# Stores of decay matrices, feed-forward blocks and scaled rows: issued by the engine that makes the data instead of SyncE

## The chip, the cores and the metric

The kernel runs on one core of one Trainium2 chip. TensorE (PE) multiplies matrices; VectorE (DVE), ScalarE (ACT) and GpSimd (POOL) work element by element; SyncE (SP) issues transfers (DMAs) between the device's memory (DRAM) and the on-chip buffer. Any of SP, ACT and POOL can issue a DMA, and each engine executes its own instructions strictly in order: an instruction that waits for a semaphore holds up everything behind it on that engine. The metric is the time of one execution in device microseconds (us), as the median of several runs.

## What is computed

The program is a two-layer network on a sequence of 1024 rows of width 1024, in float32. Each layer is a mixer (a gated delta rule, "GDN", in layer 0; retention in layer 1), a layer norm, a convolutional feed-forward network of hidden width 2816, and another layer norm. Cut to what the change touches:

```python
def conv_ffn(h, w_up, conv_w, conv_b, w_down):
    gate, up = jnp.split(h @ w_up, 2, axis=-1)
    gate = causal_dwconv(gate, conv_w) + conv_b
    return (jax.nn.silu(gate) * up) @ w_down

for i in range(DEPTH):
    sh1, sc1, g1, sh2, sc2, g2 = jnp.split(mod, 6, axis=-1)
    y = mixers[i % N_MIXERS](x * (1.0 + sc1) + sh1)
    x = layer_norm(DN_ALPHA * x + (1.0 + g1) * y, ln_g[i, 0], ln_b[i, 0])
    y = conv_ffn(x * (1.0 + sc2) + sh2, ffn_up[i], ...)
    x = layer_norm(DN_ALPHA * x + (1.0 + g2) * y, ln_g[i, 1], ln_b[i, 1])
# in the gated delta rule:
    decay = jnp.where(causal, jnp.exp(jnp.where(causal, diff, 0.0)), 0.0)
```

## The kernel before

**Stages**, by the profiled execution's time: the GDN mixer (0 to about 580 us), its output projection (to 770), feed-forward up of layer 0 (770 to 1170), feed-forward down (to 1440), retention's input projections (to 1715), retention's core (to 2040), its output projection (to 2230), a transition in which the inputs of the next product are built (to 2290), feed-forward up of layer 1 (2290 to 2690), feed-forward down (to 2840), and the last layer norm (to 2894).

**Feed-forward up** (`layer_tail`, `strassen`, `wino`). The hidden width is taken in 11 pairs `fp` of 256 columns. Each pair has a gate item and an up item, and each item is one 2x2 block product in the Strassen-Winograd form: seven products of blocks instead of eight. An item loads two weight tiles `wr` of 128x1024 (L1357 for a11 and a12, L1358 for a21 and a22); the pool holds two such tiles, so each load waits until the last reader of the same buffer is done. DVE makes sums of weight blocks (L1346, `mm<-wr`), and every weight block, raw or summed, is split into a high and a low part by ScalarE (L89) and DVE (L90) before PE multiplies with it (L110 to L112). Raw blocks appear as `wb<-wr`, summed ones as `wb<-mm`; the last read of a `wr` buffer is such a DVE split or an L1346. ScalarE also copies products (L1362, `pc`).

A gate item's results are added up into `g` (L1723), and `conv_q` makes four quarter blocks `o` from them: ScalarE scales (L1732), DVE adds two shifted rows (L1737, twice), ScalarE applies SiLU (L1738). The up item multiplies each `o` by its result (L1760). Then four more blocks S1 to S4 are made in place in the same four `o` buffers, by GpSimd (L1768) except in the first pair. The feed-forward down product will read seven blocks per pair: 11, 12, 22 and S1 to S4. Each is written to DRAM by `store` (L1749): 7 x 11 x 2 layers = 154 stores of 256 KB. The `o` buffers come from the pool `qkv` of 20 buffers, 16 of which hold the right-hand blocks during this stage, so the next pair's L1732 can only begin when a store of the present pair has landed.

**Background.** While PE multiplies, a queue of background steps loads columns of the modulation weights (`mvw`, L227) and scales the residual rows `xg` (two GpSimd instructions L411 and L412, then a store by GpSimd itself, L413).

**GDN.** `t_decay` makes one decay matrix `U` per head: ScalarE applies exp (L841), and a 512 KB store puts it into DRAM (`Ld`, L842), from which 16 reads (L1038) take it later. There are eight heads.

**Retention.** `gain_step` (16 times with a store) scales residual rows on GpSimd (L2050, L2051) and stores them (L2052). It runs between the steps of the core; there GpSimd also makes the power function of each chunk's variance (L1976), for which DVE waits.

**What sets the order.** The program is written in a planned order, but the order on each engine is set when it is built, by a list scheduler that plays the program through with its own costs for every instruction. So a changed cost on one engine can move instructions on all of them. Loads wait in SP's queue in program order.

Of the kernel before, what the change touches and what calls it, by code (L numbers as in the profile page):

```python
# [26 lines left out]
ABLK = ("11", "12", "22", "S1", "S2", "S3", "S4")  # L27
# [6 lines left out]
def trunk_kernel(ctx: ExitStack, tc, A):  # L34
    nc = tc.nc
    pe, act, dve, pool, sp = nc.tensor, nc.scalar, nc.vector, nc.gpsimd, nc.sync
# [9 lines left out]
    def tl(tag, shape, dt=F32, name=None):  # L46
        return sb.tile(shape, dt, tag=tag, name=name or tag, bufs=BUFS[tag])
# [31 lines left out]
    def flat(ap):  # L79
        return ap.rearrange("p a b -> p (a b)")  # L80

    def hs(half):
        return slice(half * HALF, (half + 1) * HALF)
# [10 lines left out]
    def after(key):  # L94
        return tc.issue_after(anchor[key].ins) if key in anchor else nullcontext()
# [295 lines left out]
    xg = [dr.tile([S, D], F32, tag=f"xg{i}", name=f"xg{i}") for i in range(3)]  # L391
# [306 lines left out]
    U, DT, R, St = {}, {}, {}, {}  # L698
# [22 lines left out]
    def after_ev(*names):  # L721
        return ("ev", names)

    def emit(name, lat=0.0):
        events[name] = clk[0] + lat
# [45 lines left out]
    def take(tag, n):  # L771
        while free[tag] < n:
            yield lambda: free[tag] >= n
        free[tag] -= n
# [40 lines left out]
    Ld = dr.tile([GH, P, S], F32, tag="Ld", name="Ld")  # L815
# [3 lines left out]
    def decay(h):  # L819
        home = "auh" if h > 3 else "t2"  # L820
        for q4 in range(2):
            yield from take(home, 2)
            gm = [tl(home, [P, 4, P], F32R, name="gm") for _ in range(2)]
            for t, g in zip(gm, (gh64, gl64)):
                pool.tensor_tensor(t, bm(m_incl, 4), bc(g[:, q4s(q4), h], P), ALU.mult)
            yield LAT["gm"]
            pt = acc_tile() if h > 3 else sc_tile()
            pm(pt, m_lowr, gm[1], start=True, stop=False)
            pm(pt, m_lowr, gm[0], start=False, stop=True)
            dve.tensor_tensor(U[h][:, q4s(q4)], v4(pt), bm(mneg, 4), ALU.add)  # L830
            give(home, 2)

    def t_decay(p):
        yield after_ev(("g",), ("DD", p - 1), ("T", p // 2 - 1))
        for h in pairs[p]:
            yield from take("aux", 1)
            U[h] = tl("aux", [P, NCH, P], name="U")
            yield from decay(h)
        yield LAT["mm"]
        for h in pairs[p]:  # L840
            act.activation(flat(U[h]), flat(U[h]), AF.Exp)  # L841
            sp.dma_start(Ld[h], flat(U[h]))  # L842
        emit(("DD", p), LAT["exp"])

    def t_path(g):
# [383 lines left out]
    c, z = "c", "z"  # L1229
# [5 lines left out]
    for p in range(4):  # L1235
        q = p & 2
        todo += [(q + 0.28, t_decay(p)), (q + 0.2, t_chain(p)), (q + 0.25, prep(p)), (q + 0.22, dt_half(p, 0)), (q + 0.24, dt_half(p, 1)),
                 (q + 0.0 + p % 2 * 0.1, scan(p, pairs[p][0])), (q + 0.05 + p % 2 * 0.1, scan(p, pairs[p][1]))]
# [442 lines left out]
    def layer_tail(i, mix, wout, xsrc, x_mid, x_out, ln_next, final):  # L1681
# [25 lines left out]
        ad = dr.tile([NF // 2, 7, P, HALF], F32, tag=f"ad{i}", name=f"ad{i}")  # L1707
# [4 lines left out]
        def pair_items(fp):  # L1712
            g, o = [], {}

            def gate_start():
                g.extend(tl("lane", [P, D], name="g") for _ in range(2))

                def gate(q, a, b):
                    dst = g[q // 2][:, hs(q % 2)]
                    if b is None:  # L1720
                        act.activation(dst, a, AF.Copy)
                    else:
                        dve.tensor_tensor(dst, a, b, ALU.add)  # L1723
                return gate

            def conv_q(q):
                f, hf = 2 * fp + q // 2, q % 2
                gv = g[q // 2]
                w = cw[:, 3 * f:3 * f + 3]
                t = tl("qkv", [P, HALF], name="o")  # L1730
                with after("sp") if fp == 0 else nullcontext():
                    act.activation(t, gv[:, hs(hf)], AF.Copy, scale=w[:, 2:3])  # L1732
                for j in (1, 2):
                    c0 = HALF if hf else j
                    c1 = HALF * (hf + 1)
                    tv = t[:, c0 - HALF * hf:]
                    dve.scalar_tensor_tensor(tv, gv[:, c0 - j:c1 - j], w[:, 2 - j:3 - j], tv, ALU.mult, ALU.add)  # L1737
                act.activation(t, t, AF.Silu, bias=cb[:, f:f + 1])  # L1738
                o[q] = t

            def conv():
                for q in (1, 3, 0, 2) if fp == 0 else range(4):
                    if fp < 2:
                        late.append(lambda q=q: conv_q(q))
                    else:
                        conv_q(q)

            def store(nm, q):
                sp.dma_start(ad[fp, ABLK.index(nm)], o[q])  # L1749

            def up_start():
                seen = []

                def gated(q, a, b):
                    while q not in o:
                        late.pop(0)()
                    c = a
                    if b is not None:
                        dve.tensor_tensor(c, a, b, ALU.add)
                    dve.tensor_tensor(o[q], o[q], c, ALU.mult)  # L1760
                    if q != 1:
                        store({0: "11", 2: "12", 3: "22"}[q], q)
                    seen.append(q)
                    if len(seen) == 4:
                        for d, x, y, op, nm in ((1, 1, 3, ALU.add, "S1"), (0, 1, 0, ALU.subtract, "S2"),
                                                (2, 2, 0, ALU.subtract, "S4"), (3, 3, 0, ALU.subtract, "S3")):
                            def one(d=d, x=x, y=y, op=op, nm=nm):
                                (dve if fp == 0 else pool).tensor_tensor(o[d], o[x], o[y], op)  # L1768
                                store(nm, d)
                            if fp == 0:  # L1770
                                late.append(one)
                            else:
                                one()
                return gated

            return [(up[4 * fp], up[4 * fp + 2], gate_start, conv), (up[4 * fp + 1], up[4 * fp + 3], up_start, None)]
# [93 lines left out]
    for t in range(4):  # L1870
        x = tl("cv", [P, 516], name="xlo")[:, 0:HALF]
# [175 lines left out]
    def gain_step(m):  # L2047
        if gx:
            x, c, rs, gb = gx.pop()
            pool.tensor_tensor(x, x, gb[0], ALU.mult)  # L2050
            pool.tensor_tensor(x, x, gb[1], ALU.add)  # L2051
            sp.dma_start(xg[0][rs, hs(c)], x)  # L2052
        if m < 2 * NCH:
            c, r = divmod(m, NCH)
            if r == 0:
                gbs.append([tl("auh", [P, HALF], name="gb") for _ in range(2)])
                for t, nm in zip(gbs[-1], ("ln_g", "ln_b")):
                    sp.dma_start(t, A[nm][1:2, hs(c)].to_broadcast([P, HALF]))
            rs = slice(r * P, r * P + P)
            x = tl("lane", [P, HALF], name="xg")  # L2060
            sp.dma_start(x, xs[1][rs, hs(c)])
            gx.append((x, c, rs, gbs[-1]))

    gbs = []
    gains += [lambda m=m: gain_step(m) for m in range(2 * NCH + 1)]
    events["core", -1] = clk[0]
    free["qkv"] = 20
# [106 lines left out]
```

## Time and profile before

| | |
|---|---|
| median of 3 runs | 2893.8 us (2892.51 to 2897.38) |
| the profiled execution | 2895.86 us, of which its span is 2894.1 us |
| PE clock | 0.989 of full speed, mean over the span |
| PE busy | 2796.1 us (97%) |
| DVE busy | 2180.7 us (75%) |
| ACT busy | 1295.6 us (45%) |
| POOL busy | 487.1 us (17%) |
| DMA | 465.30 MB, mean 161 GB/s; 42.8% of the 16 DMA engines' time in the queues that SP and ACT feed, 0.8% in the one that POOL feeds |

An engine's busy time is the time in which at least one of its recorded instructions ran, without the instructions that issue DMAs on SP and ACT, the waits and the branches. A row of a timeline is: start in us, duration in us, engine, line, operation, the tiles written and read, their shapes, and in square brackets the idle time just before the instruction and what ended it. A row of the list of waits is: the waiting engine and line, what it waited for, then the total in us, the number of waits and the longest. "SPq" is SyncE's queue of DMA issues.

### The profile page before, as it was taken

How to read it: one execution, taken by the hardware profiler on the slowest of the kernel's cores; microseconds unless marked ns; L12 is line 12 of the kernel's file. 1: busy time of each engine (PE TensorE's matmuls, PEld its weight loads, DVE VectorE, ACT ScalarE, POOL GpSimd, SP SyncE). 2: the span in 40 equal slices, each digit the busy share in tenths (PEclk: the TensorE clock that was granted, in tenths of full speed). 3: DMA queues.
4: the chain of work that ended last, by engine and by line, in shares of the span. 5: the costliest groups of instructions: out<-in, count | busy, mean ns of one | idle time of the engine just before them, and what ended most of it. 6: DMA issues, size and time to landing. Idle time of an engine off the chain costs nothing.

```text
span 2894.1 us, 38921 instructions
## 1 busy us (share of the span) xinstructions
PE 2796.1 (97%) x13594; PEld 2287.9 (79%) x13594; DVE 2180.7 (75%) x3874; ACT 1295.6 (45%) x2387; POOL 487.1 (17%) x509
## 2 busy tenths in 40 slices
PE   8999999999999999999999999999999999999997
PEld 6787888877788778887888887777777788888886
DVE  5787688676788888868687656666688887777779
ACT  4663465344654444545333342222244644444543
POOL 0311221000023233000000002333201023332001
PEclk9999999999999999999999999999999999999999
DMA  7223243164254555855343364665754154434853
GB/s 277 88 95 121 91 137 99 52 240 153 95 189 164 193 182 171 295 154 189 126 148 120 120 200 151 198 207 172 245 195 146 62 197 138 142 129 164 289 182 117
DMA packets 252884, 465.30 MB, mean 161 GB/s; under 512 B 24144, under 2 KB 77776, under 8 KB 252688
## 3 DMA queue, kind: packets, MB, share of 16 engines
q1 hardware_dynamic: 218560, 408.02, 42.8%
q10 hardware_dynamic: 31488, 46.15, 4.3%
q0 software_dynamic: 2640, 8.65, 0.8%
q8 instruction: 107, 1.75, 0.3%
q14 instruction: 89, 0.73, 0.1%
HBM read 346.86 MB, written 115.87 MB: 160 GB/s over the span
## 4 chain that ended last, share of the span: by engine, by line
PE 54%; DVE 23%; DMA 12%; ACT 5%; issue 5%; POOL 1%; SPq 0%; ACTq 0%; DVEq 0%; POOLq 0%
PE acc L716 8%; PE acc L1292 5%; PE acc L1592 4%; PE acc L110 4%; PE acc L111 4%; PE acc L112 4%; PE sc L716 4%; DMA mvw<-in_ada_w 3%; PE sc L1292 3%; PE mm L716 2%; DVE o L1737 2%; DVE wb L90 2%; DMA wr<-in_ffn_up 2%; DVE qkv L490 2%; DVE mm L1346 2%
## 5 line engine op out<-in xcount | busy, mean ns | idle before, releaser
L716 PE MATMUL acc<-hT,wh 128*128 128x512 f32 x960 | 301.3, 396 | 0.0
L1592 PE MATMUL acc<-bb,ab 128*128 128x512 f32 x984 | 232.5, 396 | 7.1 <-DVE ab L90 3.7
L89 ACT ACTIVATE ab<-ar 128x512 fp32r<-128x512 f32 x210 | 131.1, 630 | 222.8 <-PE mm L303 49.8
L1592 PEld LDWEIGHTS acc<-bb,ab 128*128 128x128 f32 x984 | 185.6, 190 | 49.0 <-DVE bb L90 4.1
L716 PEld LDWEIGHTS acc<-hT,wh 128*128 128x128 f32 x960 | 183.7, 191 | 36.1
L90 DVE TENSOR_TENSOR ab<-ar,ab 128x512 fp32r<-128x512 f32 x210 | 147.8, 710 | 83.0 <-ACT ab L89 83.0
L1292 PE MATMUL acc<-T,wb 128*128 128x512 f32 x840 | 202.0, 390 | 0.4 <-DVE wb L90 0.4
L716 PE MATMUL acc<-hT,wl 128*128 128x512 f32 x480 | 197.9, 412 | 3.5 <-ACT sq L509 2.4
L89 ACT ACTIVATE wb<-mm 128x512 fp32r<-128x512 f32 x216 | 124.3, 597 | 169.5 <-DVE mm L1346 155.2
L1292 PEld LDWEIGHTS acc<-T,wb 128*128 128x128 f32 x840 | 157.6, 188 | 33.7 <-ACT o L1738 1.2
L90 DVE TENSOR_TENSOR wl<-wr,wh 128x1024 fp32r<-128x1024 f32 x98 | 124.6, 1272 | 76.5 <-ACT wh L89 72.8
L89 ACT ACTIVATE wh<-wr 128x1024 fp32r<-128x1024 f32 x98 | 103.6, 1060 | 138.3 <-PE acc L716 53.5
L90 DVE TENSOR_TENSOR wb<-wr,wb 128x512 fp32r<-128x512 f32 x162 | 115.8, 716 | 62.9 <-ACT wb L89 62.9
L1768 POOL TENSOR_TENSOR o<-o 128x512 f32<-128x512 f32 x80 | 113.4, 1426 | 267.4 <-ACT pc L1362 176.3
L1737 DVE SCALAR_TENSOR_TENSOR o<-g,vc,o 128x512 f32<-128x512 f32 (+2 forms) x176 | 149.6, 860 | 8.6 <-ACT o L1732 7.4
L90 DVE TENSOR_TENSOR wb<-mm,wb 128x512 fp32r<-128x512 f32 x216 | 145.2, 685 | 7.6 <-ACT wb L89 7.6
L89 ACT ACTIVATE wb<-wr 128x512 fp32r<-128x512 f32 x162 | 101.1, 626 | 92.7 <-PE acc L1292 27.9
L1346 DVE TENSOR_TENSOR mm<-wr 128x512 f32<-128x512 f32 x108 | 85.8, 794 | 74.5 <-DMA wr<-in_ffn_up 60.9
L716 PE MATMUL acc<-wh,hT 128*128 128x512 f32 x384 | 134.4, 412 | 1.8 <-DVE vv L90 1.8
L1362 ACT ACTIVATE pc<-acc 128x512 f32<-128x512 f32 x143 | 84.3, 590 | 108.7 <-PE acc L1292 63.0
L239 DVE SCALAR_TENSOR_TENSOR ada<-mvw,e,ada 128x512 f32<-128x512 f32 x140 | 106.0, 757 | 26.0 <-DMA mvw<-in_ada_w 25.7
L110 PE MATMUL acc<-T,wb 128*128 128x512 f32 x292 | 114.5, 392 | 5.2 <-DVE wb L90 5.1
(674 smaller groups left out, 7369.9 us busy)
## 6 DMA issues: line engine op xcount, KB each, us to landing
wr<-in_ffn_up SPq DMA_DIRECT2D x92, 512.0 KB, 3.9
mvw<-in_ada_w SPq DMA_DIRECT2D x80, 512.0 KB, 4.3
ad<-o SPq DMA_DIRECT2D x154, 256.0 KB, 2.3
ar<-ad SPq DMA_DIRECT2D x154, 256.0 KB, 3.8
Br<-in_ffn_down SPq DMA_DIRECT2D x88, 256.0 KB, 3.4
wr<-in_ret_wv SPq DMA_DIRECT2D x32, 512.0 KB, 3.6
ar<-od SPq DMA_DIRECT2D x56, 256.0 KB, 4.8
wr<-in_gdn_wqkv SPq DMA_DIRECT2D x24, 512.0 KB, 3.6
```

The costliest lines, as they stand in the source:

```text
L89: anchor["sp"] = act.activation(dst_h, src, AF.Copy)
L90: eng.tensor_tensor(dst_l, src, dst_h, ALU.subtract)
L110: mm(acc, wl[:, k], hl[0], start=first, stop=False)
L111: mm(acc, wh[:, k], hl[1], start=False, stop=False)
L112: mm(acc, wh[:, k], hl[0], start=False, stop=last)
L239: dve.scalar_tensor_tensor(a, wr[:, kk], e[:, k:k + 1], a, ALU.mult, ALU.add)
L716: pq(pe.matmul(out, lhsT, rhs, start=start, stop=stop), cost or COST[out.shape[-1]])
L1292: return pe.matmul(*a, skip_group_check=True, **kw)
L1346: dve.tensor_tensor(t, x, y, op)
L1592: return pe.matmul(*args, skip_group_check=True, **kw)
L1737: dve.scalar_tensor_tensor(tv, gv[:, c0 - j:c1 - j], w[:, 2 - j:3 - j], tv, ALU.mult, ALU.add)
L1768: (dve if fp == 0 else pool).tensor_tensor(o[d], o[x], o[y], op)
```

## The change

Three lines name another engine as the issuer of a store. No arithmetic, no buffer and no transfer is added or taken away.

```diff
@@ t_decay
         for h in pairs[p]:
             act.activation(flat(U[h]), flat(U[h]), AF.Exp)
-            sp.dma_start(Ld[h], flat(U[h]))
+            act.dma_start(Ld[h], flat(U[h]))
         emit(("DD", p), LAT["exp"])
@@ pair_items
             def store(nm, q):
-                sp.dma_start(ad[fp, ABLK.index(nm)], o[q])
+                pool.dma_start(ad[fp, ABLK.index(nm)], o[q])
@@ gain_step
             pool.tensor_tensor(x, x, gb[0], ALU.mult)
             pool.tensor_tensor(x, x, gb[1], ALU.add)
-            sp.dma_start(xg[0][rs, hs(c)], x)
+            pool.dma_start(xg[0][rs, hs(c)], x)
```

The list scheduler moves other instructions too. GpSimd's queue over one pair of feed-forward up in layer 0 (L411 to L413 are two background gains, L1768 the blocks S1 to S4) was:

```order
L411 TENSOR_TENSOR xg<-xg,gb 128x512
L412 TENSOR_TENSOR xg<-xg,gb 128x512
L413 DMA xg_161<-xg 128x512
L411 TENSOR_TENSOR xg<-xg,gb 128x512
L412 TENSOR_TENSOR xg<-xg,gb 128x512
L413 DMA xg_161<-xg 128x512
L1768 TENSOR_TENSOR o<-o 128x512 x4
```

and is now, over the part of a pair from the first gain's store on:

```order
L413 DMA xg_161<-xg 128x512
L1749 DMA ad_6811<-o 128x512
L411 TENSOR_TENSOR xg<-xg,gb 128x512
L412 TENSOR_TENSOR xg<-xg,gb 128x512
L413 DMA xg_161<-xg 128x512
L1749 DMA ad_6811<-o 128x512
L1768 TENSOR_TENSOR o<-o 128x512
L1749 DMA ad_6811<-o 128x512 x2
L1768 TENSOR_TENSOR o<-o 128x512
L1749 DMA ad_6811<-o 128x512
L1768 TENSOR_TENSOR o<-o 128x512 x2
L1749 DMA ad_6811<-o 128x512 x2
```

The seven stores of a pair now stand in GpSimd's queue, five of them between and behind its four L1768.

On DVE, at the end of an up item in the same stage (`wb<-wr` in L90 is the split of a raw weight block, whose end lets the next item's load L1358 begin; the two L1737 are the next pair's convolution), the difference is:

```order
 L1723 TENSOR_TENSOR g<-sc,pc 128x512
 L90 TENSOR_TENSOR wb<-mm,wb 128x512
-L1737 SCALAR_TENSOR_TENSOR o<-g,vc,o 128x511
-L1737 SCALAR_TENSOR_TENSOR o<-g,vc,o 128x510
-L90 TENSOR_TENSOR wb<-wr,wb 128x512 x2
+L90 TENSOR_TENSOR wb<-wr,wb 128x512
+L1737 SCALAR_TENSOR_TENSOR o<-g,vc,o 128x511
+L1737 SCALAR_TENSOR_TENSOR o<-g,vc,o 128x510
+L90 TENSOR_TENSOR wb<-wr,wb 128x512
 L1346 TENSOR_TENSOR mm<-wr 128x512
```

The first of the two splits has moved ahead of the two L1737. The same is found in most pairs of both layers.

On ScalarE, at the same place (`mm` and `wr` as on DVE; L1732 and L1738 are the convolution's first and last step), the difference is:

```order
 L89 ACTIVATE wb<-mm 128x512 x2
-L1732 ACTIVATE o<-g,vc 128x512
-L1362 ACTIVATE pc<-acc 128x512
-L89 ACTIVATE wb<-wr 128x512
-L1738 ACTIVATE o<-o,vc 128x512
+L1362 ACTIVATE pc<-acc 128x512
+L89 ACTIVATE wb<-wr 128x512
+L1732 ACTIVATE o<-g,vc 128x512
 L1362 ACTIVATE pc<-sc 128x512
 L89 ACTIVATE wb<-wr 128x512
 L251 ACTIVATE ada,cs<-mm 128x128 x4
+L1738 ACTIVATE o<-o,vc 128x512
```

L1732, which needs an `o` buffer that a store has left, has moved behind the copy L1362 and the split L89, and L1738 behind the next pair of these.

## The prediction

> **What bounds the kernel now.** I began with the page's totals, then took the chain that ended last, then the stages in which the moved stores lie.
>
> ```profile
> span 2894.1 us, 38921 instructions
> PE 2796.1 (97%) x13594; PEld 2287.9 (79%) x13594; DVE 2180.7 (75%) x3874; ACT 1295.6 (45%) x2387; POOL 487.1 (17%) x509
> PE 54%; DVE 23%; DMA 12%; ACT 5%; issue 5%; POOL 1%; SPq 0%; ACTq 0%; DVEq 0%; POOLq 0%
> ```
>
> PE runs 97% of the span, and issuing transfers on SP is 0% of the chain. So a store that leaves SP's queue saves nothing by itself: it can win only PE's idle time, and only where a load came late because it stood behind that store. The stages (from, length, then busy us and count of PE, PEld, DVE, ACT, POOL, PE clock, DMA share, GB/s), for feed-forward up 0 and 1, retention's core, the transition and the tail:
>
> ```profile
> 770.00:1170.00 400.00, 392.85 (x1728) 319.81 (x1727) 336.81 (x519) 191.49 (x376) 106.84 (x84) 1.00 0.50 171
> 2290.00:2690.00 400.00, 398.23 (x1745) 326.89 (x1744) 319.01 (x472) 190.53 (x325) 111.77 (x88) 1.00 0.47 161
> 1715.00:2040.00 325.00, 319.38 (x1453) 247.84 (x1452) 207.11 (x367) 85.30 (x141) 98.25 (x108) 1.00 0.59 184
> 2230.00:2290.00 60.00, 53.44 (x224) 40.85 (x223) 41.03 (x65) 32.42 (x54) 1.94 (x2) 0.94 0.16 54
> 2840.00:2894.00 54.00, 38.89 (x170) 31.25 (x168) 50.84 (x102) 15.61 (x25) 13.22 (x8) 0.91 0.22 84
> ```
>
> PE is idle 7.2 us in feed-forward up 0 (400 less 392.85), 1.8 in feed-forward up 1, 5.6 in retention's core. These cap what the stages with most of the moved stores can give back. PE's waits in feed-forward up 0 are nearly all of one kind:
>
> ```profile
> PE acc L110 <- DVE wb L90: 5.1, 4, 1.5
> PE sc L110 <- DVE wb L90: 0.7, 2, 0.4
> ```
>
> Six waits, 5.8 us, each for the split of a summed weight block. One of them, put together from the timelines of SP, ACT, DVE and PE:
>
> ```profile
> 938.74 0.73 ACT L1732 ACTIVATE o<-g,vc 128x512 f32<-128x512 f32 x1 [0.56 <-DVE g L1723]
> 939.84 0.62 ACT L89 ACTIVATE wb<-wr 128x512 fp32r<-128x512 f32 x1
> 939.50 1.70 DVE L1737 SCALAR_TENSOR_TENSOR o<-g,vc,o 128x511 f32<-128x511 f32 x2 [0.24 <-ACT o L1732]
> 941.11 0.69 DVE L90 TENSOR_TENSOR wb<-wr,wb 128x512 fp32r<-128x512 f32 x1
> 941.83 0.33 SPq L1358 DMA_DIRECT2D wr<-in_ffn_up  x1
> 947.65 0.70 DVE L1346 TENSOR_TENSOR mm<-wr 128x512 f32<-128x512 f32 x1 [3.91 <-DMA wr<-in_ffn_up]
> 956.98 0.50 PE L110 MATMUL acc<-T,wb 128*128 128x512 f32 x1 [1.38 <-DVE wb L90]
> ```
>
> Read upwards: PE waits 1.38 us for a chain that began when the weights landed; DVE had stood idle 3.91 us for them; the load was issued 0.03 us after the split at 941.11 freed its buffer (941.11 + 0.69); and this split stood behind two L1737, which waited for ScalarE. No moved store is in that chain.
>
> **The stores of the feed-forward blocks: what leaves SP.** SP's own waits:
>
> ```profile
> SPq L1357 <- DVE mm L1346: 305.1, 43, 19.8
> SPq L1749 <- DVE o L1760: 215.9, 51, 9.7
> SPq L1358 <- DVE wb L90: 85.9, 50, 5.1
> SPq L1749 <- POOL o L1768: 57.8, 57, 3.7
> SPq L2052 <- POOL xg L2051: 43.3, 16, 6.3
> ```
>
> 215.9 + 57.8 us of waiting leave SP, but behind these stores the weight loads L1357 and L1358 still wait for DVE to free a buffer. They gain next to nothing: 0.
>
> **What POOL takes on.** The rows for a store that POOL issues already (duration as min, median and max in ns), for the landing from each engine (last column, us) and for the four block sums:
>
> ```profile
> L413 POOL DMA_DIRECT2D xg<-xg x32: 580/580/759, 837.2 to 2631.0; - x32
> ad<-o SPq DMA_DIRECT2D x154, 256.0 KB, 2.3
> xg<-xg POOLq DMA_DIRECT2D x32, 256.0 KB, 2.3
> 2518.14 5.61 POOL L1768 TENSOR_TENSOR o<-o 128x512 f32<-128x512 f32 x4 [1.70 <-DVE o L1760]
> 2515.86 0.58 POOL L413 DMA_DIRECT2D xg<-xg  x1 [0.30 <-POOL xg L412]
> ```
>
> POOL spends 0.58 us on an issue, plus 0.30 us when the store waits for POOL's own result; the same 256 KB land after 2.3 us either way. 170 stores x 0.58 = 99 us raise POOL from 17% to about 20%, and a pair's burst grows from 5.61 to about 9 us out of some 39. POOL's time is hidden under PE's. If that cover went, PE would wait for `o` (a rival below).
>
> [...]
>
> **The moved rows.** In the new order DVE's first `wb<-wr` split stands ahead of the two L1737, and ScalarE's matching L89 ahead of L1732. L89 can then start about when L1732 did, some 1.1 us sooner (938.74 against 939.84, and L1362's share less), and DVE's split follows it; the load is issued about 1.2 us sooner (two L1737 took 1.70, less some 0.5 that DVE now waits for L89). If all of it reaches PE, four waits of some 1.3 lose 1.2 each and the two small ones all: 4.8 + 0.7 = 5.5. Against it, the late stores now share the load's flight:
>
> ```profile
> DMA to landing us min/median/max: 3.4/4.3/6.6
> ```
>
> This is L1358's time to landing; the load above took 5.8. If it takes the worst seen, 6.6, then 0.8 of the 1.2 us is lost, so bounds are 5.5 and 4 x 0.4 + 0.7 = 2.3, or 0 if every load is slower than any seen. I take the middle of the first two, **-3.9 us**. In feed-forward up 1 there is nothing to win: the same split is in time,
>
> ```profile
> 2538.45 1.28 DVE L90 TENSOR_TENSOR wb<-mm,wb 128x512 fp32r<-128x512 f32 x2
> 2539.67 0.39 PE L110 MATMUL acc<-T,wb 128*128 128x512 f32 x1
> ```
>
> its first half ending about 2539.1, 0.6 us before PE wants it. **0**, at best -1.8.
>
> **GDN.** Eight stores of 0.326 us move to ACT:
>
> ```profile
> L842 SPq DMA_DIRECT2D Ld<-U x8: 319/326/331, 107.4 to 393.1; - x8
> L1038 SPq DMA_DIRECT2D DT<-Ld x16: 320/422/1264, 250.5 to 491.6; - x16
> ```
>
> At worst 8 x 0.326 = +2.6 us, if ACT (45% busy) were always what PE waits for. The data is read 143 us after the first store. I take **+0.3**, a tenth.
>
> **Retention.** Sixteen stores move into POOL ahead of the power function that DVE waits for:
>
> ```profile
> 1783.43 1.27 POOL L2051 TENSOR_TENSOR xg<-xg,gb 128x512 f32<-128x512 f32 x1
> 1785.47 0.55 POOL L1976 TENSOR_TENSOR mv<-mv,mhalf 128x1 f32<-128x1 f32 x1 [0.77 <-DVE mv L1975]
> ```
>
> The store needs 0.30 + 0.58 = 0.88 us and fits a gap of 0.77, the narrowest I found, but for 0.11. SP's 43.3 us of waits go with it; what loads gain is bounded by PE's idle 5.6. Bounds -5.6 and 16 x 0.88 = +14 if no store had a gap; I take **0**, since the gap row lies beside the price.
>
> **The rest of the reordering.** Tail: DVE, 50.84 of 54 us busy, gets the reads of two power results (L1523) closer behind them; POOL's eight take 13.22, 1.65 each, so 0 to +3.3; I take **+1**. Transition: PE and DVE rows change places, PE is idle 6.6 of 60; bounds -6.6 and, one weight split late in two places,
>
> ```profile
> L90 DVE TENSOR_TENSOR wl<-wr,wh 128x1024 fp32r<-128x1024 f32 x98 | 124.6, 1272 | 76.5 <-ACT wh L89 72.8
> ```
>
> 2 x 1.27 = +2.5; I take 0.
>
> **Sum:** -3.9 + 0 + 0.3 + 0 + 1 + 0 = -2.6. The profiled execution took 2895.86 us, 1.8 more than its span, which the change leaves alone: 2893.2. The median of the runs is 2.1 below the profiled one, so **2891 us**.
>
> **Rivals.**
>
> *Nothing reaches PE.* Loads land late enough to use up the 1.2 us, and the tail stays: 2894. For: a share of 0.50 of the DMA engines is already taken. Against: the store moved is the same size.
>
> *All of it is won.* 5.8 in feed-forward up 0, retention's idle 5.6: 2893.8 - 11.4 = 2882. For: SP's 43.3 us of waits on L2051 vanish in the stage with the highest DMA share, 0.59, where transfers are most sought. Against: loads there wait for buffers too.
>
> *ScalarE is held by late blocks* (slower). A store that leaves POOL late frees its `o` late; ScalarE's L1732 waits in order, with L1362 and L89 behind it, and PE behind those.
>
> ```profile
>   ACT o L1732: 6.8, 8
> 2522.06 0.73 ACT L1732 ACTIVATE o<-g,vc 128x512 f32<-128x512 f32 x1
> 2524.04 0.62 ACT L89 ACTIVATE wb<-wr 128x512 fp32r<-128x512 f32 x1
> ```
>
> Already now it waited for these stores 8 times, 0.85 us each, and 2522.06 is just when S1's store lands. From the burst at 2518.14, S1 is now made by 2518.14 + 0.58 + 1.40 = 2520.1, issued 0.30 to 0.88 later, landed 2.3 after: 2522.7 to 2523.3. L1732 now stands behind the L89 that ends at 2524.66, so 1.4 us are spare. It decides once POOL is later by more than that, as when a background gain ahead of it waits for its load. At 0.5 us over 20 pairs (11 in each layer, less the first): +10, 2904.
>
> [...]
>
> *POOL meets DVE more often.* POOL's sums, now spread out over 9 us, overlap other DVE operations:
>
> ```profile
> 2519.89 1.47 DVE L1346 TENSOR_TENSOR mm<-wr 128x512 f32<-128x512 f32 x1
> 2530.90 0.70 DVE L1346 TENSOR_TENSOR mm<-wr 128x512 f32<-128x512 f32 x1 [2.79 <-DMA wr<-in_ffn_up]
> ```
>
> Inside the burst at 2518.14 an L1346 took 1.47, outside it 0.70. One more such hit of 0.77 in each of 20 pairs, half of it past the slack, is +8: 2902. Against: the number of sums is the same, so hits move rather than multiply.
>
> **How the numbers follow.** Of a change of 0.2%, 5.8 us, a measurement of this kernel can just tell; faster is below 2888.0, slower above 2899.6. Chances: the forecast 0.34 (0.04 of it faster, 0.28 the same, 0.02 slower; its own range 2885 to 2897), nothing 0.08 (same), all won 0.28 (0.26 faster, 0.02 same), ScalarE held 0.20 (0.18 slower, 0.02 same), POOL against DVE 0.10 (0.09 slower, 0.01 same). Faster 0.30, same 0.41, slower 0.29. The range of 2880 to 2906 reaches just past both outer cases and leaves out retention without gaps, or most bounds met at once.
>
> **What would show it.** Right: the six waits of L110 on L90 in feed-forward up 0 shrink from 5.8 to about 2 us; L1358 is issued before the two L1737; L1749 takes 0.58 us on POOL and lands after about 2.3; feed-forward up 1 stays at 1.8 us of PE idle. Wrong: ACT's L1732 waiting more than 6.8 us for stores, or PE's L110 and L1292 waiting for L1362 or L89; L1749 on POOL well over 0.76 us; L1976 later behind L2052 with PE's idle time in the core above 5.6; the tail beyond 54 us by more than 3.

## The result, and the profile after

The changed kernel took 2904.03 us (median of 11 runs, 2897.93 to 2910.05), the kernel before 2896.46 (11 runs, 2886.55 to 2899.11): a ratio of 1.0031, 95% interval 1.0019 to 1.0043. The change made it slower, by some 9 us. The forecast had been 2891.

The profiled execution of the changed kernel was its fastest one: 2897.93 us, with a span of 2896.0, only 1.9 more than the span of before. So the two profiles show where the work went, but hold only part of the 9 us. PE's last matmul ends 2879.8 us after the start in both; what was lost in one stage had been won in another, and the 1.9 us lie behind it. The page of after (share of busy time, then the chain that ended last):

```profile
span 2896.0 us, 38808 instructions
PE 2796.6 (97%) x13594; PEld 2285.1 (79%) x13594; DVE 2198.8 (76%) x3874; ACT 1293.7 (45%) x2387; POOL 567.7 (20%) x679
PE 62%; DVE 19%; DMA 9%; ACT 5%; issue 4%; POOL 0%; SPq 0%; ACTq 0%; POOLq 0%; DVEq 0%
```

POOL has gone from 487.1 to 567.7 us, and DVE, to which the change gives nothing to do, from 2180.7 to 2198.8. The stages of after, in the columns of the prediction (feed-forward up 0 and 1, retention's core, the transition):

```profile
770.00:1170.00 400.00, 393.24 (x1726) 319.00 (x1725) 345.14 (x519) 190.16 (x376) 139.96 (x155) 1.00 0.51 170
2290.00:2690.00 400.00, 395.87 (x1732) 323.99 (x1731) 320.06 (x463) 186.62 (x319) 150.62 (x165) 1.00 0.48 161
1715.00:2040.00 325.00, 318.95 (x1441) 247.30 (x1440) 208.36 (x366) 83.33 (x139) 105.72 (x124) 0.99 0.59 182
2230.00:2290.00 60.00, 54.16 (x239) 41.82 (x240) 42.73 (x68) 34.66 (x59) 2.27 (x2) 1.00 0.17 61
```

Feed-forward up 0, where 3.9 us were to be won, has PE busy for 393.24 us instead of 392.85: nothing to speak of. Feed-forward up 1 has lost 2.4 us of PE (398.23 to 395.87), and since its work begins earlier in this execution, its length tells more: from the last matmul of the transition to the first of feed-forward down it took 388.3 us, against 384.8 before, 3.5 more. PE's waits in feed-forward up 1 before:

```profile
PE acc L1292 <- DVE wb L90: 1.0, 2, 0.8
PE sc L1292 <- ACT pc L1362: 0.5, 1, 0.5
PE acc L1292 <- ACT pc L1362: 0.2, 1, 0.2
```

PE's waits of after, in feed-forward up 0 and then in feed-forward up 1:

```profile
PE acc L110 <- DVE wb L90: 4.0, 4, 1.6
PE sc L110 <- DVE wb L90: 1.3, 2, 0.8
```

```profile
PE acc L1292 <- ACT pc L1362: 1.6, 3, 0.5
PE sc L1292 <- ACT pc L1362: 1.3, 2, 0.9
PE acc L110 <- DVE wb L90: 0.8, 1, 0.8
```

The six waits of 5.8 us are still six, of 5.3. In feed-forward up 1 PE now waits 2.9 us for the copies L1362, which cost it 0.7 before, and 0.8 for a split that had been in time. Each of these copies stands behind an L1738 on ScalarE, and L1738 waits for DVE's L1737, the convolution; none stands directly behind a wait for a store. The stores themselves (duration in ns as min, median, max; who waited for them; landing; the DMA view's median of landing; then the 16 stores of retention):

```profile
L1749 POOL DMA_DIRECT2D ad<-o x154: 539/542/759, 790.7 to 2684.1; - x154
...
  ACT o L1732: 26.5, 21
...
DMA to landing us min/median/max: 2.3/3.5/7.1
```

```profile
L2052 POOL DMA_DIRECT2D xg<-xg x16: 580/604/607, 1756.6 to 2033.4; - x16
```

An issue takes POOL 0.54 us, as forecast, but the block lands after 3.5 us and not 2.3. ScalarE's L1732 waits 26.5 us for stores instead of 6.8. And one group of DVE's has become slower (from the groups of instructions: busy us, mean ns, idle before; first two lines before, last two after):

```profile
L90 DVE TENSOR_TENSOR wb<-wr,wb 128x512 fp32r<-128x512 f32 x162 | 115.8, 716 | 62.9 <-ACT wb L89 62.9
L1737 DVE SCALAR_TENSOR_TENSOR o<-g,vc,o 128x512 f32<-128x512 f32 (+2 forms) x176 | 149.6, 860 | 8.6 <-ACT o L1732 7.4
L90 DVE TENSOR_TENSOR wb<-wr,wb 128x512 fp32r<-128x512 f32 x162 | 137.1, 848 | 64.4 <-ACT wb L89 64.3
L1737 DVE SCALAR_TENSOR_TENSOR o<-g,vc,o 128x512 f32<-128x512 f32 (+2 forms) x176 | 137.0, 789 | 10.8 <-ACT o L1732 9.6
```

The split of raw weights took 716 ns in the mean before and takes 848 now; the convolution's L1737 fell from 860 to 789. Something that used to lie on the convolution now lies on the split.

**The clock.** The runs of one kernel differ by 10 to 20 us, and each run lists the mean clock that PE was granted. The line fitted to the 32 runs of before beside the first four experiments has 2.24 us of span more for each 0.001 of clock less, and passes through 2894.7 at a clock of 0.988. The line of the changed kernel passes through 2900.2 there. So at an equal clock it is 5.5 us slower, give or take some 2: in the other batches the line of the kernel before passes through 2894.3 to 2896.1 there. Its mean clock, 0.9872 against 0.9876, accounts for about another 1. The rest of the 9 lies in the 11 runs of before that the result is measured against, whose mean, 2895.0, is 2.5 below that of the 32. An equal clock is not a neutral measure either: some of the stretches at half clock begin at PE's waits (in the transition of before 6.8 us of it, at a wait of 3.19 us; last section), so a part of what a wait costs may be taken out with it.

### The profile page after: what moved, and what is told of

It is laid out like the page before. It is cut to its first block, busy times and chain, and to the rows that moved or that the text cites. A ratio compares the mean times of both kernels' runs of the same rounds, so it can differ in the third digit from the quotient of the medians.

```text
span 2896.0 us, 38808 instructions
## 1 busy us (share of the span) xinstructions
PE 2796.6 (97%) x13594; PEld 2285.1 (79%) x13594; DVE 2198.8 (76%) x3874; ACT 1293.7 (45%) x2387; POOL 567.7 (20%) x679
## 4 chain that ended last, share of the span: by engine, by line
PE 62%; DVE 19%; DMA 9%; ACT 5%; issue 4%; POOL 0%; SPq 0%; ACTq 0%; POOLq 0%; DVEq 0%
PE acc L716 8%; PE acc L1292 7%; PE acc L110 5%; PE acc L111 5%; PE acc L112 5%; PE acc L1592 4%; PE sc L716 4%; PE sc L1292 3%; PE mm L716 3%; DVE wb L90 2%; DMA wr<-in_ffn_up 2%; DMA mvw<-in_ada_w 2%; PE sc L110 2%; DVE qkv L490 2%; PE sc L111 2%
## 5 line engine op out<-in xcount | busy, mean ns | idle before, releaser
L89 ACT ACTIVATE ab<-ar 128x512 fp32r<-128x512 f32 x210 | 131.2, 630 | 223.8 <-PE mm L303 48.3
L1592 PEld LDWEIGHTS acc<-bb,ab 128*128 128x128 f32 x984 | 184.2, 189 | 48.4 <-DVE ab L90 3.2
L90 DVE TENSOR_TENSOR ab<-ar,ab 128x512 fp32r<-128x512 f32 x210 | 151.6, 726 | 83.5 <-ACT ab L89 83.2
L1292 PE MATMUL acc<-T,wb 128*128 128x512 f32 x840 | 202.0, 389 | 0.4 <-DVE wb L90 0.4
L89 ACT ACTIVATE wb<-mm 128x512 fp32r<-128x512 f32 x216 | 124.4, 597 | 165.8 <-DVE mm L1346 148.8
L90 DVE TENSOR_TENSOR wb<-wr,wb 128x512 fp32r<-128x512 f32 x162 | 137.1, 848 | 64.4 <-ACT wb L89 64.3
L90 DVE TENSOR_TENSOR wl<-wr,wh 128x1024 fp32r<-128x1024 f32 x98 | 123.8, 1264 | 77.2 <-ACT wh L89 76.9
L89 ACT ACTIVATE wh<-wr 128x1024 fp32r<-128x1024 f32 x98 | 103.7, 1060 | 145.4 <-PE acc L716 60.9
L1749 POOL DMA_DIRECT2D ad<-o x154 | 84.4, 549 | 426.7 <-DVE o L1760 388.7
L90 DVE TENSOR_TENSOR wb<-mm,wb 128x512 fp32r<-128x512 f32 x216 | 144.4, 680 | 7.3 <-ACT wb L89 7.3
L1737 DVE SCALAR_TENSOR_TENSOR o<-g,vc,o 128x512 f32<-128x512 f32 (+2 forms) x176 | 137.0, 789 | 10.8 <-ACT o L1732 9.6
L89 ACT ACTIVATE wb<-wr 128x512 fp32r<-128x512 f32 x162 | 101.2, 627 | 82.9 <-PE acc L1292 19.1
L1362 ACT ACTIVATE pc<-acc 128x512 f32<-128x512 f32 x143 | 84.4, 590 | 120.4 <-PE acc L1292 66.8
L239 DVE SCALAR_TENSOR_TENSOR ada<-mvw,e,ada 128x512 f32<-128x512 f32 x140 | 113.0, 807 | 26.0 <-DMA mvw<-in_ada_w 25.6
L1523 POOL TENSOR_TENSOR mv<-mv,mhalf 128x1 f32<-128x1 f32 x24 | 27.5, 1149 | 491.1 <-DVE mv L1522 490.0
```

The source lines that it names most:

```text
L89: anchor["sp"] = act.activation(dst_h, src, AF.Copy)
L90: eng.tensor_tensor(dst_l, src, dst_h, ALU.subtract)
L239: dve.scalar_tensor_tensor(a, wr[:, kk], e[:, k:k + 1], a, ALU.mult, ALU.add)
L1292: return pe.matmul(*a, skip_group_check=True, **kw)
L1362: act.activation(t, X, AF.Copy)
L1592: return pe.matmul(*args, skip_group_check=True, **kw)
```

## The experiments

Four theories stood against each other. **A**: the loss is in the feed-forward stores. **B**: it is in retention and GDN. **P**: late blocks hold ScalarE (the third rival of the prediction; in the expectations it includes that the order chosen because of them puts POOL's sums under the weight splits). **Q**: POOL's sums meet DVE (the fourth). A further one, **C**, was that the loss is only a lower clock. Every kernel ran against the kernel before on the same chip, in five rounds; the figure given is the ratio with its 95% interval.

### One part of the change at a time

Three runs keep one of the three edits (`pool` or `act` for `sp` in one line) and undo the other two; e4 and e9 give one group of stores to ScalarE instead, and e12 keeps two edits.

> Only the 154 stores of feed-forward blocks on POOL. Theory A (the loss lies in these stores: they land later, ScalarE's L1732 waits for them, and POOL's sums meet other DVE operations): nearly the whole loss, ratio 1.002 to 1.004, the landing of ad<-o near 3.5 us instead of 2.3, ACT's L1732 waiting about 25 us for stores instead of 6.8. Theory B (the loss lies in retention and GDN, by the other two edits): ratio 1.000 within 0.001. Theory C (the loss is a lower granted clock in whichever kernel, not a wait): the times follow the mean clock of each run, about 3 us for 0.001, and spans at an equal clock are equal.

Measured: 1.0016 (1.0002 to 1.0029). Landing was 3.4 us, L1732 waited 27.3 us. At a clock of 0.988 its line passes through 2898.4, 3.7 us above before. A holds, with less than the whole loss, and the split is as slow as in the changed kernel (874 ns in the mean); C explains runs of one kernel, not the difference of two.

> Only the 16 scaled-row stores of retention on POOL. Theory A: ratio 1.000 within 0.001, since the store fits the gap before the power function. Theory B: slower by half of the loss or more, 1.0015 or above, with DVE's L1980 waiting more than 22.5 us for POOL's L1976.

Measured: 0.9975 (0.9962 to 0.9987), faster. Neither theory expected it. The scheduler had moved the transition's transposes (L439) ahead of a wait. PE's rows there, before, and then in this run:

```profile
2233.60 0.79 PE L110 MATMUL acc<-hT,wl 128*128 128x512 f32 x1 [3.19 <-DVE wl L90]
```

```profile
2228.99 0.60 PE L439 MATMUL mm<-cst,xt 128*128 128x128 f32 x4
2231.22 0.50 PE L110 MATMUL acc<-hT,wl 128*128 128x512 f32 x1 [1.64 <-DVE wl L90]
```

The wait of 3.19 us is 1.64, and the granted clock between 2230 and 2290 us is 1.00, as in the changed kernel's window above, where it was 0.94 before. That is no chance of one execution: in the eight profiles with moved transposes this wait is 1.5 to 1.7 us and no stretch at half clock follows, in the ten others it is 3.0 to 3.6 us and one follows each time. From the last matmul of retention's core to the first of feed-forward up 1 on `T` the eight take 184.2 to 185.3 us, the ten 186.4 to 189.6.

> Only the 8 decay stores on ACT; the order on PE, DVE and POOL is that of before. Theory A: ratio 1.000 within 0.001. Theory B: slower by 0.001 or more, from PE waits on ScalarE in the first 400 us, at most 2.6 us.

Measured: 1.0003 (0.9989 to 1.0017). The decay stores cost nothing that shows.

> The 154 stores on ACT instead; PE's order is that of before, DVE's nearly so. If the issue by POOL (landing 3.5 us, POOL's queue) is what costs, landing returns to 2.3 us and the time to about that of before (1.000 within 0.001), unless ScalarE's own queue becomes the bound: 154 x 0.33 = 51 us more on ACT and waits of ScalarE for DVE's L1760, up to 200 us, would show as PE waits on L89 and L1362 and a loss above 0.5%.

Measured: 1.0028 (1.0013 to 1.0043). Landing was 2.6 us and L1732 waited only 4.3 us for stores, but PE waited 4.4 us for L1362 in feed-forward up 0 alone. ScalarE is no better place: there the stores of S1 to S4 wait for POOL's sums (L1768) in ScalarE's own queue, and the copies behind them.

> The 16 scaled-row stores of retention issued by ACT: the orders on PE, DVE and POOL are those of the kernel before, SP's is that of the second run here (e2_xg_pool). If e2 was faster because its scheduler moved the transposes of the transition ahead (a stall of 3.35 us became 1.84, and a clock dip of some 3 us was gone), this one gains nothing: 0.999 to 1.001. If e2 was faster because SP's queue no longer waits for these rows, this one gains as much: 0.997 to 0.998.

Measured: 1.0002 (0.9989 to 1.0014). With SP freed in the same way but PE's and DVE's order that of before, nothing is won. So what e2 won did not come from SP's queue; the moved instructions remain.

> The whole change without its feed-forward stores: decays on ACT, scaled rows on POOL. If the parts add up, it is as fast as e2_xg_pool, 0.9975 to 0.9985, and the feed-forward stores cost about 0.5% within the change; if they do not, about 1.000.

Measured: 0.9994 (0.9980 to 1.0008). PE and DVE run in e2's order, and its gain is not seen again, though the two intervals overlap between 0.9980 and 0.9987. A gain of 0.1 to 0.2% fits both; its size stays open. Nor do the parts add up: 1.0016 (e1) times 0.9994 is 1.0010, against 1.0031 for the whole; with an uncertainty of some 0.2% on the difference, that stays open too.

### Does the late block hold ScalarE?

One more buffer for the `o` blocks, in the changed kernel and in the kernel before:

```diff
-    BUFS = {"hTa": 8, "hTb": 8, "qkv": 20, "aux": 4,
+    BUFS = {"hTa": 8, "hTb": 8, "qkv": 21, "aux": 4,
```

> The changed kernel with one buffer more in the pool of the o blocks (21 for 20), so that the next pair's L1732 needs no store of this pair to land. Theory P (late blocks hold ScalarE, and the order that was chosen because of them puts POOL's sums under the weight splits): ACT's L1732 waits under 5 us for stores instead of 26.5, the split wb<-wr of L90 is no longer slowed to 848 ns in the mean, feed-forward up 1 is within 1 us of before, and the time is no longer above that of the next kernel, which has the same buffer without the change: ratio of the two 0.998 to 1.001. Theory Q (POOL's issues and sums cost DVE by themselves, with or without the buffer): it stays 0.2 to 0.3% above the next kernel.

> The kernel before with one buffer more in the pool of the o blocks: the control for the run ahead. ACT's L1732 waited only 6.8 us for stores before, so both theories expect 0.998 to 1.001 of the kernel before.

Measured: e5 1.0029 (1.0017 to 1.0042), e6 0.9996 (0.9987 to 1.0006). L1732's waits for stores are gone in both (1.1 and 0.9 us), and a loss of the same size is still there, now in feed-forward up 0. P falls as the main cause. The split is at 761 ns in e5, against 717 in e6: slowed much less than in the changed kernel, but where it counts. Seven loads stand behind the waits of L110 in feed-forward up 0 of e5, and six of them were released by a raw split of 1.77 or 1.78 us; in e6 all six were released by one of 0.68 or 0.69. (Neither has the moved transposes.) One place shows how, since DVE runs the same order there, with the split behind the L1737 in both. POOL's sums, DVE's split and SP's load of the next weights, in e5:

```profile
1032.94 3.01 POOL L1768 TENSOR_TENSOR o<-o 128x512 f32<-128x512 f32 x2
1034.73 1.77 DVE L90 TENSOR_TENSOR wb<-wr,wb 128x512 fp32r<-128x512 f32 x1
1036.53 0.33 SPq L1358 DMA_DIRECT2D wr<-in_ffn_up  x1
1051.16 0.50 PE L110 MATMUL acc<-T,wb 128*128 128x512 f32 x1 [2.46 <-DVE wb L90]
```

and in e6, same pair:

```profile
1022.01 6.25 POOL L1768 TENSOR_TENSOR o<-o 128x512 f32<-128x512 f32 x4
1028.73 0.68 DVE L90 TENSOR_TENSOR wb<-wr,wb 128x512 fp32r<-128x512 f32 x1
1029.43 0.33 SPq L1358 DMA_DIRECT2D wr<-in_ffn_up  x1
1044.78 0.50 PE L110 MATMUL acc<-T,wb 128*128 128x512 f32 x1 [1.44 <-DVE wb L90]
```

In e6 the four sums run in one piece and end at 1028.26, before the split starts; the split takes 0.68 us. In e5 stores stand between the sums, the last of them lies over the split, and the split takes 1.77. The load goes out as soon as the split is done in both. The split is 1.09 us longer, and PE's wait behind it 1.02 us (2.46 against 1.44).

### Which stores, and is it the sums?

> The change, but the three product blocks of a pair (11, 12, 22) are stored by SP as before, only S1 to S4 by POOL. DVE keeps the two L1737 ahead of the split. Theory P: the sums' stores alone still land late, L1732 waits 10 to 25 us for them, but no split is moved under POOL's sums: wb<-wr near 720 ns, half of the loss or less (ratio 0.998 to 1.001, with the gain of the transition in it). Theory Q: POOL's sums are just as spread out, so the loss stays, 1.002 or above.

> The change, but S1 to S4 are stored by SP as before and only the product blocks by POOL. DVE has the split ahead of the two L1737, as in the changed kernel. Theory P: stores of sums land after 2.3 us again, L1732 waits under 15 us, but the split is under POOL's sums: wb<-wr stays above 800 ns, the load behind it stays late, half of the loss or more remains in feed-forward up. Theory Q: half of the stores have left POOL, so about half of the loss.

The edit of e7, and of e8 with the engines exchanged:

```diff
-                pool.dma_start(ad[fp, ABLK.index(nm)], o[q])
+                (pool if nm[0] == "S" else sp).dma_start(ad[fp, ABLK.index(nm)], o[q])
```

Measured: e7 1.0001 (0.9989 to 1.0014), with the split at 710 ns; e8 0.9993 (0.9980 to 1.0007), with the split at 786 ns. Neither half shows a loss against the kernel before, though both have the moved transposes and what these win; the loss does not follow the number of stores. e7 came out as P expected (no split under the sums, no loss), and not as Q did; but L1732 waited 33.1 us for stores there, more than in the changed kernel, and 3.6 us of PE's waits in its profile are for copies L1362 that stand directly behind such a wait. So late blocks can cost something. e8 fits neither expectation: its splits are slowed by half as much as in the changed kernel, and no half of the loss shows.

Next, the sums were taken out. All L1768 of e5 and e6 are left out but those of a layer's first pair, so that the four blocks are stored unsummed:

```diff
-    (dve if fp == 0 else pool).tensor_tensor(o[d], o[x], o[y], op)
+    if fp == 0:
+        dve.tensor_tensor(o[d], o[x], o[y], op)
```

> e5_after_21 without GpSimd's 80 sums S1 to S4 (the four blocks are stored without being summed in all pairs but the first of a layer; the output is not the reference's). POOL still issues all the stores. Its control is the next run, with the same order on PE. If the loss of e5 against e6 (0.33%) comes from POOL's sums, spread out by the issues, lying under DVE's weight splits, it is gone here: 1.000 within 0.001 of the next run. If it comes from the issue on POOL, from the later landing or from the traffic of the late stores, it stays: 1.002 to 1.004 of the next run.

> e6_before_21 without the same 80 sums (the output is not the reference's): the control of the run ahead. POOL's sums hit DVE's convolution there and rarely a weight split, so it should be within 0.2% of e6: 0.997 to 1.001 of the kernel before.

Measured: 0.9954 (0.9938 to 0.9969) and 0.9940 (0.9921 to 0.9960), 0.14% apart where e5 and e6 were 0.33%. That lies between the two expectations: some 4 us remain, and with an uncertainty of about 0.25% the pair is not told apart from no loss, nor from the whole one. The control missed its expectation too: without the sums the kernel before is 0.56% faster than e6, far more than 0.2%. The scheduler ordered it anew, so not all of these 16 us need be the sums, but they cost something even where they stood.

> The kernel before, stores on SP, with one tiny GpSimd addition (128x1, some 0.6 us) at the place of each of the 154 stores, reading the block that is stored: GpSimd's sums are pushed apart as in the change, and no store is issued by GpSimd. If the sums under the weight splits make the loss: 1.0015 to 1.004 of the kernel before, with wb<-wr of L90 above 770 ns in the mean. If the issue by GpSimd and the later landing make it: 1.000 within 0.001.

```diff
                 sp.dma_start(ad[fp, ABLK.index(nm)], o[q])
+                k1 = tl("s8", [P, 4], name="kk")
+                pool.tensor_tensor(k1[:, 0:1], o[q][:, 0:1], o[q][:, 0:1], ALU.add)
```

Measured: 1.0011 (0.9998 to 1.0024). This one is inconclusive. The sums were pushed apart, but only in two halves, and DVE kept the convolution ahead of the split, which stayed at 707 ns. It did not make the condition that it was to test.

Last, all the work is kept, but DVE makes the sums:

```diff
-    (dve if fp == 0 else pool).tensor_tensor(o[d], o[x], o[y], op)
+    dve.tensor_tensor(o[d], o[x], o[y], op)
```

> The kernel before with all sums S1 to S4 on DVE (80 more there, 0.6 us each at issue, 48 us in feed-forward up, where DVE is 80 to 84% busy). DVE's hits by the sums go: if these were worth more than the 24 us a layer that DVE gets, it is faster, 0.996 to 0.999; if DVE becomes the bound, 1.002 to 1.01.

> The change with all sums on DVE. If GpSimd's sums make the loss, it is equal to the run ahead within 0.1% (or ahead of it by the 0.1 to 0.2% that the reordered transition gives); if the issue by GpSimd and the landing make it, 0.2 to 0.4% slower than the run ahead.

> e2_xg_pool (scaled rows on POOL, the other stores on SP) with all sums on DVE. If both gains hold and add up, 0.1 to 0.25% faster than e14; otherwise equal to it.

Measured: e14 0.9982 (0.9968 to 0.9995), e15 0.9965 (0.9951 to 0.9979), e16 0.9982 (0.9967 to 0.9997). With the sums on DVE, the change is not slower than the kernel without it but, if anything, faster (0.17%, with an uncertainty of 0.19%), while POOL still issues all 170 stores. A loss of 0.31% is well outside that. (e15 has the moved transposes, as the changed kernel has, and e14 not.) e16 equals e14, so e2's gain does not show on top of the moved sums. Feed-forward up 0 of e14, then both feed-forward up stages of e15:

```profile
770.00:1170.00 400.00, 396.09 (x1748) 323.87 (x1747) 351.31 (x560) 194.22 (x382) 56.45 (x48) 1.00 0.52 173
770.00:1170.00 400.00, 397.94 (x1768) 328.34 (x1767) 357.14 (x569) 200.48 (x388) 93.55 (x119) 1.00 0.51 173
2290.00:2690.00 400.00, 398.74 (x1754) 328.56 (x1753) 330.98 (x517) 191.19 (x326) 97.45 (x125) 1.00 0.48 163
```

PE is busy 397.94 us in feed-forward up 0, 5.1 more than before and 4.7 more than after. Of the 5.1, 3.2 come with the sums' move alone (e14) and 1.9 with the change, so the gain that was forecast is there only in part. The six waits of L110 for a split are gone.

The profiles, put side by side: PE's waits of more than 0.15 us in the two stages (from the first L110 on `T` to the first L301), and of the loads behind L110's waits for a split, how many were released by a raw split of more than 1 us:

| | up 0, us | up 1, us | loads behind a slowed split |
|---|---|---|---|
| before | 7.0 | 1.7 | 0 of 6 |
| after | 6.6 | 4.7 | 5 of 6 |
| e1 | 6.0 | 6.1 | 5 of 6 |
| e5 (its control e6) | 14.9 (8.8) | 2.9 (2.1) | 6 of 7 (0 of 6) |
| e7 | 8.6 | 3.5 | 0 of 6 |
| e8 | 7.7 | 1.0 | 3 of 6 |
| e10 (its control e11) | 3.6 (2.4) | 2.1 (2.1) | 0 of 2 (none) |
| e15 (its control e14) | 1.2 (3.9) | 1.0 (1.0) | none (0 of 3) |

e15 is the version that beats both kernels, by 0.35% the one before and by some 0.66% the changed one (0.9965 by 1.0031). It is not shown to beat e14, whose interval it overlaps.

## Why the prediction was wrong

**What failed is the step "The moved rows", with its -3.9 us, and the 0 given to feed-forward up 1 beside it.** Feed-forward up 0 kept its six waits, at 5.3 us for 5.8, and feed-forward up 1 took 3.5 us more. The step took the new place of the split, ahead of the two L1737, at the split's old price, and weighed only the late stores' traffic against it. It did not ask what POOL does at that moment. The new place lies under the sums, which the stores push back. In the changed kernel (POOL, then DVE, then SP, then PE):

```profile
2559.39 2.54 POOL L1768 TENSOR_TENSOR o<-o 128x512 f32<-128x512 f32 x2
```

```profile
2559.80 2.70 DVE L90 TENSOR_TENSOR wb<-wr,wb 128x512 fp32r<-128x512 f32 x1 [1.87 <-ACT wb L89]
```

```profile
2562.52 0.33 SPq L1358 DMA_DIRECT2D wr<-in_ffn_up  x1
```

```profile
2575.68 0.50 PE L110 MATMUL acc<-T,wb 128*128 128x512 f32 x1 [0.75 <-DVE wb L90]
```

A split of 0.69 us takes 2.70 and ends 0.57 us after the sums (2561.93), the load that it holds back goes out 0.02 us later, and PE waits 0.75 us at the end of that chain. Over both stages, 34 raw splits overlap computing on POOL in the changed kernel, at 1.47 us in the mean, against 16 at 0.96 before; those that overlap none take 0.69. Under the sums lie 16 of the 34, at 1.89 us; before, none did. (The other 18, and the 16 of before, lie under the scaling of residual rows, L411 and L412.) The excess over 0.69 grew from 4.3 to 26.4 us. That used up the 1.2 us a pair by which the load was to go out sooner: of the five loads behind the six waits in feed-forward up 0, four were released by a split of 2.37 to 2.79 us, and the waits came to 5.3 us where some 2 were forecast. In feed-forward up 1 it used up the slack of 0.6 us too, but only in the one pair above. PE's waits grew by 3.0 us there, 2.3 of them for copies behind the convolution; e7 has 1.1 us of such waits without any slowed split, so that part stays open. e5 with e6 show the chain from sum to PE's wait; e15 with e14 show that the loss goes when the sums leave POOL, and e10 with e11 do not contradict it. Since every such edit reorders the engines, e8 fits only in part, and one profile is all there is of each kernel, how much of the loss runs through the split is not shown.

**The rival that came true** was "POOL meets DVE more often", at 2902 us, given a chance of 0.10. The argument against it, that hits move rather than multiply, was half right: L1737 lost 12.6 us of busy time (149.6 to 137.0) while the split gained 21.3 (115.8 to 137.1). Over all of DVE, the time that instructions under a sum took beyond the same ones without one rose from 29 to 40 us. But what a hit cost depended on where it lay. On the split, which frees a weight buffer, it delayed a load: in the rows above by the 2.01 us that the split took beyond 0.69. How much of a hit on the convolution was slack is not shown.

**The rival "ScalarE is held by late blocks"** got twice that chance, and its sign was seen, 26.5 us of waits. It was not the main cause: without these waits (e5) a loss of the same size was there, and in the changed kernel PE waits for no copy that stands directly behind one. But it is not free, as the 3.6 us in e7 show.

**What the stores cost by themselves.** The issue was priced rightly (0.58 forecast, 0.54 measured; POOL 20%). The landing was not: 3.5 us for 2.3. The row of 32 single gains was the wrong neighbour, since the blocks come in pairs: of the 154, the 56 issued within 1.5 us after another POOL store landed after 4.8 us in the median, the other 98 after 3.0. This mattered little.

**Retention and GDN** were right at 0 to 0.3 as far as the runs can tell: DVE waits 21.6 us for L1976 instead of 22.5, PE's idle time in the core is 6.1 us instead of 5.6, and e3 shows no cost. The **transition**, taken at 0 between -6.6 and +2.5, was a gain: from the core's last matmul to the first of feed-forward up 1 on `T`, 185.3 us instead of 189.2, of which 3.4 had been lost to 6.8 us at half clock that it no longer has. The prediction left the clock out there, though its row shows 0.94. The **tail**, at +1, was 1.9 us longer in the profiles, all of it after PE's last matmul.

**The sum** of what the profiles show at an equal clock is smaller than the 5.5 us of the runs' lines; one profile of each kernel does not resolve the rest, and it stays open, as does the 0.14% between e10 and e11.

## What to carry to other kernels

A store that is moved to a busy engine's queue also moves that engine's own work: ask where each of its instructions will now lie, and what the engine whose instructions took longer beside them (here DVE: 1.89 us for 0.68) is doing there. Price a moved instruction at its new neighbours, not at its old mean, and look first at instructions that free a buffer, since a load waits for each. Where one kernel's runs differ by more than the change, look at their granted clock too, and at where it fell: in the transition of before it was 0.81 between 2226 and 2244 us, around a wait of 3.19 us, and a comparison at an equal clock would leave out what that lower clock cost.

## What the runs showed of the hardware

**DVE beside POOL's sums.** DVE instructions with both inputs in SBUF, the on-chip buffer, took longer in the mean under POOL's 128x512 sums: in the changed kernel 1.89 us (16 `wb<-wr`, up to 3.00) for 0.68 beside no computing on POOL, and 1.10 (16 `mm<-wr`) for 0.70; before, 1.29 (21 L1737) for 0.75. Those with one input in PSUM, the buffer that PE writes its products to in this kernel (`wb<-mm`), did not: 0.68 us both beside computing on POOL (50 in the changed kernel) and without (166). Of the 16 raw splits under sums, 13 began while a sum ran; they took 1.13 to 3.00 us, and each ended some 0.56 us after the end of a sum, as the split of 2.70 us above did. The other three began 0.14 to 0.65 us before the sum and took 0.69. With the 80 sums given to DVE (e14), 80 x 0.69 = 55 us of work, DVE's page shows only 19.3 us more,

```profile
PE 2794.0 (97%) x13594; PEld 2286.7 (79%) x13594; DVE 2200.0 (76%) x3954; ACT 1297.4 (45%) x2387; POOL 377.3 (13%) x429
```

which is 36 us less than that work. In the profile of before, the instructions that overlapped a sum took 29 us longer than the same ones without; that this makes up most of the 36 is the author's estimate.

**Stretches at half clock.** In the profiles of before and after, the granted clock is 1 but for stretches at 0.5, of 3.41, 6.83 or 10.24 us (the last one, of 11.34 and 13.95, begins after PE's last matmul). Of the ten ahead of that one in before, eight begin during one of PE's waits of 0.8 us or more or at most 4.5 us behind it; of the nine in after, seven. But most such waits have none: 27 of 35 in before, 28 of 35 in after. At the transition's longest wait, between 2226 and 2244 us, one follows in all ten profiles where the wait is 3.0 to 3.6 us, and in none of the eight where it is 1.5 to 1.7; near 700 us three waits of 0.9, 1.0 and 1.4 us stand in all eighteen profiles, and nine show such a stretch there, nine none (the clock between 685 and 703 us is 0.81 in after and 1.00 in before). So a wait can come with more lost time than its length: with the 3.19 us in the transition of before come 6.83 us at half clock, 3.4 us of full speed as an estimate, and in e2, where the wait is 1.64, they are gone too. What decides whether a stretch follows a wait is not shown.
